# Two head pairs walk their WKV chunks together; low-rank products are made once, ahead of the heads

## The chip, the cores and the metric

One core of a Trainium2 chip runs the whole program, in one launch. The metric is the time of one execution on the device in microseconds; the kernel before takes 1480.89 us in the median of three runs (1479.6 to 1481.0).

## What is computed

The reference is one layer of a decoder for 512 prompt tokens and 8 samples of 8 tokens each, 576 columns in all: a SwiGLU feed-forward block, a mixing block, and a second feed-forward block. The mixing block has three branches (an RWKV-7 recurrence, a causal convolution, a cross-attention), each weighted by its own sigmoid gate, summed and projected. The change lies in the RWKV branch. Cut to that:

```python
wd, ad, gd = xm[..., c3:c4], xm[..., c4:c5], xm[..., c5:]           # 64, 64 and 160 wide
w_log = -jax.nn.softplus(-(p['w0'] + jnp.tanh(wd) @ p['w_decay_up'])) - 0.5
decay = jnp.exp(-jnp.exp(w_log))
a = jax.nn.sigmoid(p['a0'] + ad @ p['w_a_up'])
g = jax.nn.sigmoid(gd) @ p['w_g_up']
...
def step(s, inp):                                                    # per head, 64 x 64 state
    sa = jnp.einsum('bhij,bhj->bhi', s, -kk_t)
    s = (s * w_t[:, :, None, :] + sa[..., None] * kka_t[:, :, None, :]
         + v_t[..., None] * k_t[:, :, None, :])
    return s, jnp.einsum('bhij,bhj->bhi', s, r_t)
...
y_a = (o.reshape(b, t, D_RWKV) * g) @ p['w_rwkv_out']
```

There are 8 heads of 64 channels, handled as 4 pairs of 128 channels (one pair fills the 128 partitions).

## The kernel before, in words

Channels lie on partitions and the 576 tokens in the free dimension, in two halves of 288. A large product is made of three matmuls in the type fp32r: each operand is split into a rounded part and the rest (`split`, a ScalarE cast at L96 and a VectorE subtraction at L97), and the rest times the rest is left out. These matmuls are issued at L110 (`mm3k`, called by `proj`), 24 for each half and 1024 input channels, and at L382 in the feed-forward blocks. Small products are single matmuls in plain fp32, which the profile counts as two passes each (transposes as one).

The mixing block starts when the first feed-forward block ends. `lora` makes the inputs of three low-rank products (`la`, `lg`) by the projections 12, 13 and 14 of `w_in`. Then the string `PLAN` gives the order in which the pieces are written down, and the scheduler of the tile framework settles the order of each engine from it: A is the attention, P`j` the preparation of pair `j` (`prep`), I`j` the inverse of the 32 x 32 triangles (`inverse`, mostly VectorE), J`j` their joining into 64 x 64 (`joined`), B`j` the recurrence of pair `j` (`chain`), G and C the convolution, and X, Y, Z are the 24 gates, each a projection of 48 matmuls at L110 that depends on nothing else of the mixing. The gates fill TensorE while the other pieces wait for VectorE, ScalarE and each other.

`prep` makes in plain fp32 the products of `la` with `wda` for decay and for `a` (L128, `full`), and the masked Gram blocks (L893). `chain` transposes `kb` and `v` (L911, L915), runs `chunks`, then `sample_chunk`, and then the norm over each head. In the norm, the sums of squares are spread to all rows by matmuls at L148, and the product of `lg` with `wg` follows (L128 again, bank `c`); its result in PSUM multiplies the normed output. `chunks` walks the 8 chunks of 64 tokens of a pair one after the other. A chunk is one bank of PSUM and these matmuls, all for the two heads of one pair: values (L1024), the state's share (L1027), the solve (L1031), the update of the state (L1042), the output (L1057) and the state's share of the output (L1059). Between them stand two ScalarE copies (`xs` L1029, `vu` L1033), a scaled copy of the state (`mg` L1047) and VectorE's update (`st` L1051). The next chunk's L1027 needs the updated state.

Outputs of pairs 0 to 2 go to memory (`d_ya`) and come back before the merge, which multiplies all four by `w_rwkv_out`; its matmuls are the first at L110 that read `k`, `r`, `av`, `zt`, `w`, `g` and `u1`.

PSUM has three banks with the tag `p`, two with `g` and three with `c`. All loads and most stores are issued by SP's queue, in the order that the scheduler sets. Weights are loaded at L86 (`w<-win` and others) into two buffers of 1024 columns.

## Time and profile before

| what | value |
|---|---|
| median of three runs | 1480.89 us |
| the profiled execution, whole | 1484.21 us |
| its span, first to last instruction | 1482.4 us |
| its mean granted TensorE clock | 0.985 |
| TensorE busy | 1464.2 us, 10820 matmul passes |
| VectorE busy, ScalarE busy | 1026.1 us, 676.2 us |
| the mixing block up to the merge, about | 421 to 994 us of the span |

A page of the profile gives the busy time of each engine, the chain of waits that ended last, and groups of instructions by line. A busy TensorE is not a TensorE at its peak: a matmul's end is modelled, and a row's length covers its passage through the array. The distance from the start of one row to the start of the next tells what it held the engine for. "128*64" in a row is the part of the array that is used, rows by columns.

### The profile page before, as it was taken

Reading aid. Unit: us, or ns where it says so; the run is one execution under the profiler, and the core shown is the slowest. Engines: PE = TensorE matmul, PEld = TensorE weight load, DVE = VectorE, ACT = ScalarE, POOL = GpSimd, SP = SyncE. Lnnn points to the kernel's source line nnn. Section 1 sums busy time; section 2 is a strip of 40 time slices with the busy share of each in tenths; the row PEclk is TensorE's granted clock in tenths of the full one; section 3 lists DMA queues with packets and bytes.
Section 4 is the critical chain, followed back from the end, with each engine's and each line's share of the span. In section 5 each row is a group of like instructions: output and inputs, shape, how many; then the busy total and the mean of one; then the engine's idle time right before and its main releaser. Section 6 shows DMA issues by size and latency. Waiting matters only on the chain.

```text
span 1482.4 us, 27100 instructions
## 1 busy us (share of the span) xinstructions
PE 1464.2 (99%) x10820; PEld 1382.3 (93%) x10820; DVE 1026.1 (69%) x2054; ACT 676.2 (46%) x1371; POOL 4.7 (0%) x22
## 2 busy tenths in 40 slices
PE   9999999999999999999999999999999999999998
PEld 9999999999998799878889878789999999999997
DVE  7976777777783569769456456357578766777775
ACT  7443434444577535445446533443354433444342
POOL 0000000000010000000000000000000000000000
PEclk9999999999999989999999999999999999999999
DMA  6222222233632244123223124345322322323221
GB/s 210 72 80 92 87 86 86 86 91 102 202 105 86 65 132 83 55 80 105 62 61 109 55 85 137 96 161 189 102 73 72 100 73 85 100 89 98 86 86 65
DMA packets 95179, 144.06 MB, mean 97 GB/s; under 512 B 43645, under 2 KB 53501, under 8 KB 95053
## 3 DMA queue, kind: packets, MB, share of 16 engines
q1 hardware_dynamic: 94476, 141.74, 31.1%
q8 instruction: 85, 1.39, 0.4%
q10 hardware_dynamic: 576, 0.59, 0.1%
q14 instruction: 42, 0.34, 0.1%
HBM read 126.07 MB, written 16.23 MB: 96 GB/s over the span
## 4 chain that ended last, share of the span: by engine, by line
PE 92%; DVE 4%; ACT 1%; DMA 1%; issue 1%; SPq 0%; DVEq 0%; POOL 0%; ACTq 0%; POOLq 0%
PE p L110 51%; PE p L382 26%; PE c L1027 1%; PE g L893 1%; PE c L1031 1%; PE c L1024 1%; DVE pr L986 1%; PE c L128 1%; PE c L1059 1%; PE g L128 1%; PE c L1057 1%; DVE cc L676 1%; PE c L1079 1%; DVE tt L988 1%; PE c L1042 1%
## 5 line engine op out<-in xcount | busy, mean ns | idle before, releaser
L110 PE MATMUL p<-x,wh 128*128 128x288 f32 x3136 | 655.6, 300 | 1.3 <-ACT kv L562 0.7
L110 PEld LDWEIGHTS p<-x,wh 128*128 128x128 f32 x3136 | 507.2, 189 | 15.2 <-issue 7.1
L110 PE MATMUL p<-x,wl 128*128 128x288 f32 x1568 | 470.0, 300 | 1.5 <-DVE wl L97 1.5
L96 ACT CAST wh<-w 128x512 fp32r<-128x512 f32 (+1 forms) x353 | 209.8, 600 | 261.9 <-PE p L382 99.8
L97 DVE TENSOR_TENSOR wl<-w,wh 128x512 fp32r<-128x512 f32 (+1 forms) x353 | 232.4, 663 | 117.4 <-ACT wh L96 110.4
L110 PEld LDWEIGHTS p<-x,wl 128*128 128x128 f32 x1568 | 295.4, 189 | 7.1 <-issue 3.1
L382 PE MATMUL p<-t,wh 128*128 128x288 f32 x1088 | 224.3, 298 | 0.0
L382 PEld LDWEIGHTS p<-t,wh 128*128 128x128 f32 x1088 | 173.8, 188 | 6.4 <-DVE t L393 6.4
L382 PE MATMUL p<-b,wh 128*128 128x288 f32 x816 | 169.7, 295 | 0.0
L382 PE MATMUL p<-t,wl 128*128 128x288 f32 x544 | 160.6, 295 | 0.0
L96 ACT CAST wh<-p 128x512 fp32r<-128x512 f32 x136 | 84.5, 621 | 156.1 <-PE p L110 117.7
L382 PEld LDWEIGHTS p<-b,wh 128*128 128x128 f32 x816 | 132.6, 188 | 0.0
L97 DVE TENSOR_TENSOR wl<-p,wh 128x512 fp32r<-128x512 f32 x136 | 93.7, 689 | 50.1 <-ACT wh L96 47.4
L382 PE MATMUL p<-b,wl 128*128 128x288 f32 x408 | 120.3, 295 | 0.0
L382 PEld LDWEIGHTS p<-t,wl 128*128 128x128 f32 x544 | 102.4, 188 | 0.0
L382 PEld LDWEIGHTS p<-b,wl 128*128 128x128 f32 x408 | 76.8, 188 | 0.0
L460 DVE SCALAR_TENSOR_TENSOR x<-p,x 128x288 f32<-128x288 f32 x128 | 57.9, 453 | 20.0 <-PE p L110 19.9
L96 ACT CAST x<-t 128x576 fp32r<-128x576 f32 (+1 forms) x60 | 36.5, 610 | 45.0 <-DVE t L464 41.8
L1051 DVE SCALAR_TENSOR_TENSOR st<-c,gc,mg 64x64 f32<-64x64 f32 x56 | 15.9, 284 | 53.3 <-PE c L1042 52.5
L372 DVE TENSOR_TENSOR p<-w 128x512 f32<-128x512 f32 x68 | 46.7, 687 | 4.2 <-DMA w<-wu 3.8
L372 DVE TENSOR_TENSOR p<-p,w 128x512 f32<-128x512 f32 x68 | 46.5, 683 | 0.2 <-DMA w<-wu 0.2
L676 DVE SCALAR_TENSOR_TENSOR cc<-up,pv,cc 128x512 f32<-128x512 f32 x60 | 43.9, 750 | 0.1
(354 smaller groups left out, 1990.8 us busy)
## 6 DMA issues: line engine op xcount, KB each, us to landing
w<-wu SPq DMA_DIRECT2D x85, 512.0 KB
w<-win SPq DMA_DIRECT2D x44, 512.0 KB
w<-wd SPq DMA_DIRECT2D x64, 256.0 KB
w<-wd SPq DMA_DIRECT2D x16, 384.0 KB
d_mb<-gate SPq DMA_DIRECT2D x16, 288.0 KB
w<-wo SPq DMA_DIRECT2D x8, 512.0 KB
d_x<-x SPq DMA_DIRECT2D x16, 144.0 KB
d_g<-gate SPq DMA_DIRECT2D x8, 288.0 KB
```

Source lines behind the costliest of these rows:

```text
L96: self.A.copy(hi, x)
L97: self.V.tensor_tensor(lo, x, hi.bitcast(F32), ALU.subtract)
L110: self.T.matmul(p, l, x[r][:, c], start=k == 0 and i == 0, stop=k == n - 1 and i == 2)
L128: self.T.matmul(p, l, r[:, c], start=i == 0, stop=i == len(ops) - 1)
L372: V.tensor_tensor(s, u, v, ALU.add)
L382: self.T.matmul(p, hl[l][:, c], xs[k][b][:, o], start=first and k == 0 and q == 0, stop=k == 3 and q == 2, skip_group_check=True)
L460: V.scalar_tensor_tensor(x[m][:, c], p, 0.5, x[m][:, c], ALU.mult, ALU.add)
L676: V.scalar_tensor_tensor(c[:, :SEQ], up[:, k:k + SEQ], w, c[:, :SEQ], ALU.mult, ALU.add)
L893: T.matmul(ps[:, i * 128:(i + 1) * 128], kb[o, c + i].rearrange("p a t -> p (a t)"), ra[o, c + i].rearrange("p a t -> p (a t)"), start=Tru ...
L986: V.tensor_tensor(pr, tt[:, :n, :e].unsqueeze(2).broadcast_to([np_, n, m, e]), l3[:, t:e, :e].unsqueeze(1).broadcast_to([np_, n, m, e]), A ...
L988: V.tensor_reduce(tt[:, :n, t:e], pr, op=ALU.add, axis=AX.X)
L1051: V.scalar_tensor_tensor(mn[s, s], ps[s, 256 + 64 * h:320 + 64 * h], gc[s, c:c + 1], mg[s, s], ALU.mult, ALU.add)
```

## The change

The four recurrences become two: `chains(j)` takes pairs `j` and `j + 1` and walks both through each chunk together. One bank holds values, share of the state, solve and update of both; `xs` and `vu` are copied once, 256 wide; the outputs of both go to a bank of tag `g`. The state update is four products of 64 columns of `kbt` (L1143) instead of one of 128 columns for each pair. The values of the next chunk are issued right after the outputs. The sample chunk of each pair is cut into three pieces, and one piece is issued behind each of the first six chunks. The order of the matmuls within a chunk is partly fixed by `keep_in_program_order`.

The transposes move from the recurrence into `prep` (bank `g`). All low-rank products move to the beginning (`low_rank`): they become fp32r matmuls in parts (L677, 64 of 288 columns), and their results go to memory (`d_w`, `d_a`, `d_gt`) and are loaded where they are needed. For this `wda` is loaded twice over both halves of the partitions, and the 32 last rows of `lg` are made three times (96 rows in projection 14). `PLAN` is new. Only pairs 0 and 1 go to memory before the merge.

```diff
-PLAN = ("A0 P0 I0 Y3 G0 J0 P1 B0 Y1 I1 X2 Y1 X2 J1 P2 B1 "
-        "X1 I2 X2 C0 Y3 P3 J2 B2 X1 Z1 I3 Z3 J3 B3 Z2 L0 Z2")
+PLAN = ("A0 P0 I0 Y3 G0 P1 J0 I1 Y3 X1 J1 B0 X3 P2 I2 Y2 X2 P3 J2 X2 I3 C0 Z2 J3 B2 Z4 L0 Z2")
...
+    def low_rank(self, zp):
+        ...
+        def products(*ops):
+            for h in range(2):
+                c = slice(h * H, (h + 1) * H)
+                p = self.bank("g")[:, :H]
+                for q, (l, r) in enumerate(ops):
+                    T.matmul(p, l, r[:, c], start=q == 0, stop=q == len(ops) - 1)
+                yield c, p
+        for j in range(4):
+            ...
+                for c, p in products((wh[:, i, ch], xs[:, i]), (wl[o, ch], xs[o, i])):
+                    A.activation(t[:, c], p, AF.Sigmoid, bias=self.par(par, j))
+                self.store(out[j], t)
+            ...
+            for c, p in products((gh[:, 0, ch], lg[:, 0]), (gh[:, 0, ch], lg[:, 1]), (gl[:, ch], lg[:, 0]),
+                                 (gh[:96, 1, ch], gs[:96])):
+                A.copy(t[:, c], p)
+            self.store(self.d_gt[j], t)
...
-        for c, p in self.full("g", (self.wda[:64, 128 * j:128 * j + 128], self.la[:64])):
-            A.activation(sg[:, c], p, AF.Sigmoid, bias=par("w0", j))
+        self.dma(sg, self.d_w[j])
...
-        ch = slice(128 * j, 128 * j + 128)
-        for c, p in self.full("c", (self.wg[0][:, ch], self.lg[0]), (self.wg[1][:, ch], self.lg[1])):
-            V.tensor_tensor(rs[:, c], p, rs[:, c], ALU.mult)
+        gt = b3.tile([128, N], F32, name="gt")
+        self.dma(gt, self.d_gt[j])
+        V.tensor_tensor(rs, gt, rs, ALU.mult)
...
+    def chains(self, j):
+        samples = [s for i in (j, j + 1) for s in self.sample_chunk(i)]
+        self.chunks(j, lambda: samples and samples.pop(0)())
+        for i in (j, j + 1):
+            self.mixed(i)
...
+            xs = self.b3.tile([128, 256], F32, name="xs")
+            A.copy(xs[64:], ps[64:, :256])
+            for i, h, s in parts:
+                T.matmul(ps[64:, col(0, i, h)], made[i][0][64:, h, c, 64:], xs[64:, col(0, i, h)], start=True, stop=True)
+            A.copy(vb[64:, c].rearrange("p i v -> p (i v)"), ps[64:, :256])
+            for i, h, s in parts:
+                gr, kbt, vu, ra, gc, bv = made[i]
+                T.matmul(ps[s, 256 + 64 * i:320 + 64 * i], kbt[:, c, s], vu[:, c, s], start=True, stop=True)
+            mn = self.st[c % 3]
+            py = self.bank("g")
```

Three places show how the program's order moves. The first is TensorE within a chunk. Before, in the recurrence of pair 0, from one chunk's share of the state (L1027) to its update (L1042); L110 are the matmuls of a gate:

```order
L1027 MATMUL c<-st_5310,ra 64x128
L110 MATMUL p<-x_4953,wh 128x288
L110 MATMUL p<-x_4954,wh 128x288
L110 MATMUL p<-x_4953,wl 128x288
L1024 MATMUL c<-vu,gr 64x64 x2
L110 MATMUL p<-x_4955,wh 128x288
L1031 MATMUL c<-xs,gr 64x64 x2
L110 MATMUL p<-x_4956,wh 128x288
L110 MATMUL p<-x_4955,wl 128x288
L110 MATMUL p<-x_4957,wh 128x288
L1042 MATMUL c<-vu,kbt 128x128
L110 MATMUL p<-x_4958,wh 128x288
```

Now, in the recurrence of pairs 0 and 1, from the end of a run of gate matmuls (here at L109) over the update (L1143), the outputs (L1151, L1153), the next chunk's values (L1122) and a piece of a sample chunk (L1201) to the next share of the state (L1132):

```order
L109 MATMUL p<-x_4958,wh 128x288
L109 MATMUL p<-x_4957,wl 128x288
L1143 MATMUL c<-vu,kbt 64x64 x4
L1151 MATMUL g<-gr,vu 64x64 x2
L1153 MATMUL g<-ra,st_5315 128x64
L1151 MATMUL g<-gr,vu 64x64 x2
L1153 MATMUL g<-ra,st_5315 128x64
L1122 MATMUL c<-vu,gr 64x64 x4
L1201 MATMUL c<-u_8005,kbt 64x512
L1201 MATMUL c<-u_8008,kbt 64x512
L1132 MATMUL c<-st_5316,ra 64x128 x2
```

The groups have twice the matmuls, update, outputs and values stand together without a gate between them, and the gate matmuls stand in three runs.

The second is SP's queue behind the first recurrence. Before, around the store of pair 0's output (`d_ya_100`) and the next loads of weights:

```order
L809 DMA d_mb_85<-gate 128x576
L86 DMA w<-woc 128x256
L941 DMA d_ya_100<-u_7459 128x576
L86 DMA w<-win 128x1024
L248 DMA d_g_96<-gate 128x576
```

Now, with the stores of pairs 0 and 1 (`d_ya_100`, `d_ya_101`), the loads of `gt` (one buffer) and the next weights:

```order
L85 DMA w<-win 128x1024 x2
L1000 DMA d_ya_100<-u_8235 128x576
L996 DMA gt<-d_gt_113 128x576
L1186 DMA ms<-wst 64x8x64 x2
L863 DMA d_mb_89<-gate 128x576
L1000 DMA d_ya_101<-u_8271 128x576
L85 DMA w<-win 128x1024
```

A load of weights stands behind two stores and a load that wait for the end of the norms of both pairs.

The third is TensorE behind the last norm. Now, from pair 3's spread (L147) through the last gate matmuls:

```order
L147 MATMUL g<-cst,u_10747 128x128 x4
L147 MATMUL g<-cst,u_10747 128x64
L109 MATMUL p<-cb0h,wh 128x288
L109 MATMUL p<-cb0l,wh 128x288
L109 MATMUL p<-cb0h,wl 128x288
L109 MATMUL p<-cb1h,wh 128x288
L109 MATMUL p<-cb1l,wh 128x288
L109 MATMUL p<-cb1h,wl 128x288
```

Twelve matmuls of the last gate stand there (six are shown), then eleven of the merge that read pairs 0 to 2, and the next reads pair 3. Before, four matmuls at L128 and 44 at L110 stood between that spread and the merge.

## The prediction

> **What bounds the kernel now.** The page comes first: its busy times and the chain that ended last.

> ```profile
> span 1482.4 us, 27100 instructions
> PE   1464.2 (99%) x10820; PEld 1382.3 (93%) x10820; DVE 1026.1 (69%) x2054; ACT 676.2 (46%) x1371; POOL 4.7 (0%) x22
> PE 92%; DVE 4%; ACT 1%; DMA 1%; issue 1%; SPq 0%; DVEq 0%; POOL 0%; ACTq 0%; POOLq 0%
> ```

> TensorE is busy 99% and carries 92% of the chain. So the first question is what the change makes TensorE do, and only then who waits. The change touches the mixing block alone, so next come the stretches of that block (span, TensorE busy, weight loads, VectorE, ScalarE, GpSimd, granted clock, DMA share, GB/s), and the chain's own rows where gate and merge matmuls run dense.

> ```profile
> 421.00:994.00 573.00, 563.13 (x4103) 489.22 (x4102) 354.64 (x809) 284.04 (x663) 4.26 (x15) 0.96 0.32 92
> 720.00:740.00 20.00, 19.89 (x128) 16.15 (x128) 5.50 (x14) 8.85 (x21) 0.00 (x0) 0.83 0.17 46
> 1438.42 22.22 PE p L110 x168
> ```

> A dense fp32r matmul of 288 columns holds TensorE for 22.22/168 = 0.132 us. In the mixing TensorE is idle in only 10 of 573 us, but it isn't dense: the small matmuls hold it much longer than their columns need. The timeline of one chunk of pair 0 shows how (start, length, line; the distance between starts is what counts).

> ```profile
> 621.04 0.34 PE L1057 MATMUL c<-gr,vu 128*64 128x64 f32 x4
> 621.30 0.43 PE L1059 MATMUL c<-ra,st 128*128 128x64 f32 x2
> 621.67 0.43 PE L1027 MATMUL c<-st,ra 128*64 128x128 f32 x2
> 622.03 0.53 PE L110 MATMUL p<-x,wh 128*128 128x288 f32 x2
> 622.40 0.29 PE L110 MATMUL p<-x,wl 128*128 128x288 f32 x1
> 622.62 0.44 PE L1024 MATMUL c<-vu,gr 64*64 64x64 f32 x4
> 622.99 0.40 PE L110 MATMUL p<-x,wh 128*128 128x288 f32 x1
> 623.32 0.44 PE L1031 MATMUL c<-xs,gr 64*64 64x64 f32 x4
> 623.69 0.40 PE L110 MATMUL p<-x,wh 128*128 128x288 f32 x1
> 623.93 0.30 PE L110 MATMUL p<-x,wl 128*128 128x288 f32 x1
> ...
> 624.20 0.40 PE L1042 MATMUL c<-vu,kbt 128*128 128x128 f32 x2
> 624.36 0.38 PE L110 MATMUL p<-x,wh 128*128 128x288 f32 x1
> 624.58 0.29 PE L110 MATMUL p<-x,wl 128*128 128x288 f32 x1
> ...
> 625.60 0.28 PE L1057 MATMUL c<-gr,vu 128*64 128x64 f32 x2
> ```

> From L1057 to the next L1057 are 4.56 us, with fifteen matmuls of L110 in them, which dense would take 15 x 0.132 = 1.98 us. The chunk step therefore holds TensorE for 2.58 us. The two groups of 64*64 take 0.37 us each, and the first gate matmul behind a group 0.24 (623.69) or 0.33 (622.99) instead of 0.132: each change of the part of the array that is used costs 0.1 to 0.2 us.

> Does the recurrence's own chain of waits limit it instead? Two rows of the groups say no: TensorE waited 0.4 us in all for the updated state, VectorE's update 52.5 us for TensorE.

> ```profile
> L1057 PE MATMUL c<-gr,vu 128*64 128x64 f32 x128 | 10.9, 249 | 0.4 <-DVE st L1051 0.4
> L1051 DVE SCALAR_TENSOR_TENSOR st<-c,gc,mg 64x64 f32<-64x64 f32 x56 | 15.9, 284 | 53.3 <-PE c L1042 52.5
> ```

> **The change part by part.** *Low-rank products.* Those of decay and `a` go from `prep`, those of `g` from behind the norm; the second row below is one of four pairs'.

> ```profile
> L128 PE MATMUL g<-la,wda 64*128 64x288 f32 x32 | 9.4, 442 | 0.5 <-ACT u L827 0.5
> 984.34 2.72 PE c L128 x8
> ```

> Removed: 9.4 + 4 x 2.72 = 20.3 us. Added: 64 fp32r matmuls of 288 columns, dense 64 x 0.132 = 8.5 us. Sixteen of them use 64 rows of the array and stand between others that use 128. At 0.1 us for the way in and 0.1 out they cost 3.2 us more, at 0.2 each 6.4 us, at nothing 0. I take 3.2, since a group that keeps the columns and changes the rows is nearer to the cheap switches. Gain 8.6 us, bounds 5.4 and 11.8. [...]

> *Chunks of two pairs together.* Thirty-two single steps become sixteen double ones. A double step has twice the passes, but most groups keep one switch. What a pass adds inside a group is shown by runs of equal passes: ten of L1027 in 1.23 us, 0.12 each, and those of 64*64 at 0.06.

> ```profile
> 636.80 1.31 PE L1027 MATMUL c<-ms,ax 128*64 128x128 f32 x10
> 638.03 0.44 PE L1031 MATMUL c<-xs,gr 64*64 64x64 f32 x4
> 752.08 0.22 PE L1024 MATMUL c<-vu,gr 64*64 64x64 f32 x1
> 752.14 0.22 PE L1024 MATMUL c<-vu,gr 64*64 64x64 f32 x1
> ```

> To 2.58 us come: values 4 x 0.06, solve 4 x 0.06, share of the state 2 x 0.12, that is 0.72; outputs a second time with their switch, 0.26 + 0.37 = 0.63; and the update, now eight passes of the form of L1057, whose four take 0.26, so 0.52 instead of the 0.25 that its two held TensorE (0.38 from 624.20 to 624.58, less one L110), 0.27 more. The double step holds TensorE 4.20 us, two single ones 5.16: 0.96 saved, sixteen times 15.4 us. Two of the sixteen are first steps without state terms, and pieces of sample chunks stand inside some groups and split them, so I take 12 us; the bounds are 0 (each doubled group costs double) and 15.4. The halved ScalarE copies (`xs`, `vu`) gain nothing by themselves: ScalarE is at 284 of 573 us in this block. The rest of the step's waits gets more cover, since the fillers per double step stay about fifteen.

> *Transposes.* The same 72 on the same engine, now in a bank of `g` instead of `c`; 0 us. Gate matmuls hide the copies; without that cover two banks instead of three cost up to the length of a copy, twelve times for each kind, which I count below.

> *The beginning.* Sixteen sigmoids and eight copies out of PSUM and the splits move to where the mixing starts; two banks of `g` serve all of them.

> ```profile
> L827 ACT ACTIVATE u<-g,pv 128x288 f32<-128x288 f32 x8 | 3.9, 501 | 2.3 <-PE g L128 2.2
> 440.00:460.00 20.00, 20.00 (x137) 17.77 (x135) 6.85 (x17) 11.13 (x28) 0.53 (x1) 1.00 0.41 135
> ```

> Twenty-four at about 0.5 us are 12 us of ScalarE. It has 9 us free in those 20, and the products and the projections between them last about 28 us by count (118 gate or projection matmuls, 15.6, and 11.7), so it fits with little room. I take 2 us lost, bounds 0 and 8 (the 12 us less half the free time).

> *The end.* Before, the last low-rank product and 31 gate matmuls stood between pair 3's spread and the merge. Now twelve do, and eleven of the merge itself: 23 x 0.132 = 3.0 us of cover.

> ```profile
> 987.05 4.32 PE p L110 x31
> L935 DVE TENSOR_TENSOR u<-u,bv 128x576 f32<-128x576 f32 x4 | 3.0, 748 | 0.6 <-ACT u L934 0.6
> L97 DVE TENSOR_TENSOR u<-u,u 128x576 fp32r<-128x576 f32 x1 | 0.8, 759 | 0.7 <-ACT u L96 0.7
> ```

> Behind the spread come six operations over 576 columns in a row (scale, affine, sum, gate, cast, rest), at about 0.75 us each 4.5 us. 1.5 us are late; bounds 0 and 4.5.

> *SP's queue.* A load of weights now stands behind the stores of both pairs' outputs and behind `gt`, whose one buffer is free only after the first norm; the gate matmuls behind it on TensorE wait. The longest wait for weights in this block, on the chain of waits, is the upper bound:

> ```profile
> 575.33 7.71 DMA w<-win
> ```

> With the banks of `g` I take 2 us, bounds 0 and 8.

> Sum: -8.6 - 12 + 2 + 1.5 + 2 = -15.1 us. The profiled execution took 1484.21 us (1482.4 in the span and 1.8 around it), 3.3 more than the median of 1480.89. The sum holds for either: 1469.1 for an execution like the profiled one, and 1480.9 - 15 = 1466 us for the median, my forecast.

> **The rivals.** *Slower: the clock.* Between 720 and 740 us TensorE is busy 19.89 of 20 us and is granted 0.83 of its clock; dense stretches have 1.00. So small matmuls without enough dense ones between them lower the clock, and over the block 0.04 of 573 us is lost, some 20 us. The change packs the small groups: update, outputs and values stand together, and a sample piece among them. A double step with fifteen fillers lasts 4.20 + 1.98 = 6.2 us, sixteen 99 us. If 0.83 held in all of them, they would take 99/0.83 = 119 us, 20 more than forecast: 1486 us. It decides below a mean of 0.87 in these stretches (99/114). Against it: a double step has a third of its time in dense matmuls, and the single step of 4.56 us that is shown has not much more. [...]

> *No change: the groups don't share.* If each doubled group costs double, only the low-rank products gain, and the beginning, the end and the queue take most of it: -8.6 + 5.5 = -3.1, 1478 us; with a little more lost it is no change. For it speaks that every switch between parts of the array remains inside the outputs; against it the 0.06 and 0.12 us above.

> *Less gain: ScalarE bounds the beginning, or the queue starves TensorE.* At one of the ends of 8 us the total is 1472 us.

> *More gain.* Chunk steps at 15.4 us, nothing lost at either end, and half of the 10 us in which TensorE is idle in this block gone: -8.6 - 15.4 - 5 = -29, 1452 us.

> **How the numbers follow.** About 0.2% (3 us) can be told from no change. Chances: the forecast within 1459 to 1470, 0.42; less gain, 1470 to 1478, 0.23; more gain, 0.14; no change, 0.07; slower by the clock, 0.14. Faster: 0.79. The range leaves out the half of "more" beyond its own value and most of "slower", and takes in the no-change case: 1452 to 1482 us.

> **What would show it.** Right: the products at L677 hold TensorE 11 to 12 us in all; from one update at L1143 to the next are about 6 us, with fifteen gate matmuls, 4.2 us after their dense time; TensorE idle no more than 15 us in the mixing; clock about 0.96 there. Wrong: a clock under 0.87 around the two recurrences (the slower rival), a double step of over 5 us beside its fillers (no sharing), idle TensorE of 5 us or more before the attention (ScalarE) or behind the first recurrence (SP's queue).

## The result and the profile after

The changed kernel takes 1493.23 us in the median of six runs (1489.63 to 1500.19) against 1481.05 (1479.6 to 1484.77): a ratio of 1.0088, 95% interval 1.0059 to 1.0118. It is slower, and 27 us from the forecast of 1466. Its profiled execution took 1491.07 us, that of before 1484.21.

The page of the changed kernel, the same three rows as shown of before:

```profile
span 1489.2 us, 27301 instructions
PE   1449.4 (97%) x10884; PEld 1384.6 (93%) x10884; DVE 1028.1 (69%) x2059; ACT 664.4 (45%) x1348; POOL 5.0 (0%) x22
PE 90%; DVE 6%; issue 1%; ACT 1%; DMA 1%; SPq 0%; DVEq 0%; POOL 0%; ACTq 0%; POOLq 0%
```

TensorE is busy 14.8 us less, and the span is 6.8 us longer. VectorE has 6% of the chain instead of 4%. The stretches of the changed kernel (columns as before: span, TensorE, weight loads, VectorE, ScalarE, GpSimd, clock, DMA share, GB/s) say where:

```profile
420.00:1001.00 581.00, 549.34 (x4166) 492.37 (x4164) 356.49 (x812) 272.13 (x637) 1.55 (x4) 0.94 0.33 98
704.00:760.00 56.00, 56.00 (x513) 45.11 (x511) 18.50 (x44) 19.48 (x64) 0.00 (x0) 0.97 0.14 38
840.00:860.00 20.00, 14.39 (x74) 13.93 (x75) 11.82 (x23) 10.49 (x15) 0.00 (x0) 0.71 0.32 79
860.00:880.00 20.00, 14.48 (x137) 13.75 (x136) 8.57 (x30) 5.86 (x13) 0.00 (x0) 0.76 0.42 120
900.00:920.00 20.00, 11.44 (x119) 10.71 (x120) 4.11 (x8) 4.17 (x10) 0.00 (x0) 0.75 0.44 115
917.00:980.00 63.00, 62.54 (x516) 50.48 (x513) 23.71 (x55) 22.58 (x67) 0.00 (x0) 0.85 0.20 53
```

In the block TensorE is idle 31.7 us (581 less 549.3; before 9.9) and has 0.94 of its clock (before 0.96). Most of the idle time gathers between the first recurrence (704 to 760 us, never idle, clock 0.97) and the second (917 to 980, hardly idle, clock 0.85). The windows at half clock lie more widely: they cost 35.8 us in the block by half their length, 15 of these between the two recurrences and 12 from 917 us on. TensorE's longest waits in the block (us in total, times, longest), first of the changed kernel, then of before:

```profile
PE p L109 <- DVE wl L96: 6.7, 5, 3.2
PE c L1067 <- DMA aux<-s: 6.1, 1, 6.1
PE p L109 <- ACT cb0h L95: 5.4, 1, 5.4
```

```profile
PE c L1008 <- DMA aux<-s: 2.0, 1, 2.0
PE p L110 <- DVE wl L97: 1.5, 3, 1.1
```

L1067 is the joining of pair 3, which needs pair 3's inverse. `wl` is the rest part of a gate's weights: VectorE makes it, so the fillers themselves queue up behind the inverse's operations there. Pieces of the chain of waits ahead of it (start, length, what):

```profile
828.70 0.55 DVE pr L1045
...
850.79 0.72 DVE pr L1045
...
856.23 0.66 ACT cb0h L95
...
882.21 0.65 DVE pr L1045
...
909.38 3.07 DMA aux<-s
912.49 1.93 PE c L1067 x32
```

VectorE makes the inverse of pair 2 (816 to 852 us) and then that of pair 3 (873 to 901). Before, the inverse of pair 3 (863 to 912 us) went on beside the recurrence of pair 2 (840 to 884) and its norm. Now both inverses, the joinings and the convolution's tail (`cb0h`) must be done before the second recurrence starts.

To see all of it at once, I split the mixing, from its first matmul to the merge, in three: idle time (distances between the starts of two matmuls of over 0.9 us, each less one dense matmul), time lost at half clock (half the length of the windows at 0.5, as far as TensorE was not idle in them, so that nothing counts twice), and the rest, which is work. It is an estimate from the starts of the matmuls and the granted clock in the traces: in the mixing of the changed kernel a dense gate matmul holds TensorE 0.133 us at 1.00 and 0.240 at 0.50 (medians of 1,923 and 93), so such matmuls lose 0.45 of a window's length, a little less than half. Medians are those of each kernel's runs; the profiled times belong to the split.

| kernel | median | profiled | mixing | half clock | idle | rest |
|---|---|---|---|---|---|---|
| before | 1481.05 | 1484.21 | 571.8 | 18.3 | 10.9 | 542.5 |
| changed | 1493.23 | 1491.07 | 580.0 | 29.6 | 33.3 | 517.1 |
| changed_again | 1501.72 | 1505.83 | 594.0 | 46.3 | 31.1 | 516.6 |
| low_rank_alone | 1498.79 | 1501.11 | 588.0 | 29.6 | 22.1 | 536.3 |
| pairing_alone | 1519.99 | 1521.28 | 604.6 | 49.9 | 30.3 | 524.5 |
| two_inverses | 1478.96 | 1486.73 | 574.1 | 40.1 | 15.4 | 518.6 |
| fewer_terms | 1467.87 | 1471.02 | 559.2 | 22.5 | 21.5 | 515.3 |

The rows changed, changed_again and two_inverses have the same work on TensorE, and their rest agrees within 2 us. The work fell by 25.4 us, more than the 20.6 forecast. Idle time rose by 22.4 and half clock by 11.3: the mixing is 8.2 us longer.

### The profile page after: what moved, and what is told of

It is laid out like the page before. It is cut to its first block, busy times and chain, and to the rows that moved or that the text cites. A ratio compares the mean times of both kernels' runs of the same rounds, so it can differ in the third digit from the quotient of the medians.

```text
span 1489.2 us, 27301 instructions
## 1 busy us (share of the span) xinstructions
PE 1449.4 (97%) x10884; PEld 1384.6 (93%) x10884; DVE 1028.1 (69%) x2059; ACT 664.4 (45%) x1348; POOL 5.0 (0%) x22
## 4 chain that ended last, share of the span: by engine, by line
PE 90%; DVE 6%; issue 1%; ACT 1%; DMA 1%; SPq 0%; DVEq 0%; POOL 0%; ACTq 0%; POOLq 0%
PE p L109 50%; PE p L384 26%; DVE pr L1045 2%; DVE tt L1047 1%; PE g L945 1%; DVE wl L96 1%; PE g L677 1%; PE c L1122 1%; PE g L1153 1%; PE c L1139 1%; PE g L137 1%; DVE cc L730 1%; PE c L1086 1%; PE g L147 1%; PE c L1132 1%
## 5 line engine op out<-in xcount | busy, mean ns | idle before, releaser
L109 PE MATMUL p<-x,wh 128*128 128x288 f32 x3136 | 653.7, 301 | 4.2 <-ACT wh L95 3.5
L109 PEld LDWEIGHTS p<-x,wh 128*128 128x128 f32 x3136 | 511.8, 191 | 12.4 <-ACT wh L95 4.2
L109 PE MATMUL p<-x,wl 128*128 128x288 f32 x1568 | 472.0, 302 | 6.8 <-DVE wl L96 6.7
L109 PEld LDWEIGHTS p<-x,wl 128*128 128x128 f32 x1568 | 298.5, 191 | 12.9 <-DVE wl L96 8.7
L96 DVE TENSOR_TENSOR wl<-w,wh 128x512 fp32r<-128x512 f32 (+1 forms) x354 | 232.5, 662 | 109.8 <-ACT wh L95 99.5
L96 DVE TENSOR_TENSOR wl<-p,wh 128x512 fp32r<-128x512 f32 x136 | 93.6, 688 | 50.6 <-ACT wh L95 47.8
L851 ACT ACTIVATE gate<-p 128x288 f32<-128x288 f32 x48 | 19.7, 410 | 55.9 <-PE p L109 50.6
```

The source lines that it names most:

```text
L96: self.V.tensor_tensor(lo, x, hi.bitcast(F32), ALU.subtract)
L109: self.T.matmul(p, l, x[r][:, c], start=k == 0 and i == 0, stop=k == n - 1 and i == 2)
L851: self.A.activation(g[:, c], p, AF.Sigmoid)
```

## Experiments

**The two halves alone.** In `low_rank_alone` the recurrences and `PLAN` are those of before; in `pairing_alone` the low-rank products are (loaded in slices, for room):

```diff
-        self.dma(sg, self.d_w[j])
+        for c, p in self.full("g", (wda[:64], self.la[:64])):
+            A.activation(sg[:, c], p, AF.Sigmoid, bias=par("w0", j))
```

> The kernel before with the low-rank part of the change alone: products once at the beginning in fp32r, their results through memory, the order of the pieces and the single-pair recurrences as before. Cover theory (the loss comes from the pairing, which takes away the recurrence that covered the last inverse): the products of L677 hold TensorE 14 us as in the changed kernel, so 20.3 - 14.1 = 6 us are saved, 2 to 3 us go at the start of the mixing and 1 to 2 us at its end: 1476 to 1480 us, against 1481 before; idle TensorE in the mixing stays under 16 us. Beginning theory (ScalarE's work at the beginning and the loads and stores of its results on SP's queue make the loss): 1488 us or more, with 20 us or more of idle TensorE. Clock theory: as the cover theory, since the recurrences are as before.

> The changed kernel with the low-rank products as before (plain fp32, in the preparation and behind the norm, their weights loaded in slices for each pair), and u2 in two buffers instead of three. The first four experiments brought down the theory that only the last inverse's lost cover counts, since the low-rank part alone cost 18 us. Front theory: the low-rank products, 28 us of TensorE's order at 444 to 472 us and 16 sigmoids, 8 copies and the splits on ScalarE and VectorE, stand ahead of pair 0 in the chain of pieces; its Gram blocks come 21 us later (499 to 520 us) and its joining 33 us (575 to 608). Then without them Gram is back near 500, J of pair 0 near 580, and the time is 1493 less some 18: 1468 to 1480 us. Cover theory alone (the pairing loses): 1488 us or more.

Measured: 1498.79 us (ratio 1.0126, 1.0093 to 1.0159) and 1519.99 (1.0260, 1.0227 to 1.0293). My cover theory missed the first, and the front theory, formed on the first, missed the second: pair 0's joining did come back to 574 us, and the time rose. The work behaves as a sum: 542.5 before, 536.3 with low-rank products changed (-6.2), 524.5 with pairing (-18.0), 517.1 with both (-25.4). The time does not. Each half alone loses 18 and 39 us, the two together 12. Idle time rises by 11.2 and 19.4 us in the halves, half clock by 11.3 and 31.6. So neither half "costs" a fixed amount. That each shifts work away from where it covered a wait would fit this, but the halves alone don't show it; `pairing_alone` also has less room (`u2` in two buffers, weights loaded for each pair), and that was not separated. In `low_rank_alone` the 64 products stand at 444 to 472 us, ahead of pair 0; its joining comes at 608 us instead of 575, and all later ones 12 to 23 us later. In `pairing_alone` the plain fp32 products of `g` stand behind each recurrence, at the end uncovered: the last four hold TensorE from 1023 to 1028 us, right ahead of the merge at 1029 (changed: merge at 1001).

`half_front` moves only the products of decay and `a`:

> The changed kernel with the products of decay and a at the beginning as changed (32 of the 64), those of g as before behind the norm. Front theory: half the delay, Gram of pair 0 near 510 and its joining near 590 us, and the time between pairing_alone's and the changed kernel's: 1478 to 1488 us. If the delay comes from elsewhere (the loads of decay and a through memory): Gram at 518 to 522 and 1488 to 1496.

Measured 1506.53 us (1.0151, 1.0096 to 1.0205). Gram came at 503 to 514 us, but the joining of pair 0 only at 600. The time lies between the changed kernel's and `pairing_alone`'s, as expected, but `pairing_alone` turned out to be the slow end, and the expected 1478 to 1488 us are missed. The front theory is dropped.

**Is removed work saved?** The same kernel as before, with less in the gates:

```diff
+        self.terms = 3 - i % 2
         for c, p in self.proj(self.a["win"][20 + 8 * n + i], self.xn):
```

> The kernel before with less work on TensorE and nothing else moved by hand: in 12 of the 24 gates the third of the three products (the rest of the weights times the input) is left out, 192 matmuls of 0.132 us, 25.3 us of the mixing. If what is taken from TensorE comes off the time in full, as the prediction's sum had it: 1456 us (1452 to 1460). If the chain of pieces (VectorE's inverses, ScalarE, loads) stands close behind TensorE, a third or more comes back as idle time or as half clock: 1464 to 1476 us, and idle and half clock in the mixing rise from 31 us to 40 or more.

Measured 1467.87 us (0.9910, 0.9888 to 0.9933). Of 25.3 us taken from TensorE 13.2 came off. The block and TensorE's longest wait in it:

```profile
421.00:981.00 560.00, 542.69 (x3907) 468.01 (x3906) 352.77 (x809) 281.84 (x662) 4.26 (x15) 0.95 0.32 93
PE c L1013 <- DMA aux<-s: 3.6, 1, 3.6
```

By the split, idle time rises from 10.9 to 21.5 us and half clock from 18.3 to 22.5, and the longest wait is again the one for the last inverse. This needs no pairing and no new order: a 99% busy TensorE had other chains close behind it.

**The chain ahead of the second recurrence.** The odd pairs' inverse gets free buffers:

```diff
-        lt = b1.tile([128, 1024], F32, name="lt")[:np_]
+        lt = self.room(j, "lt", "kb", 1152)[:np_, :1024]
```

> The changed kernel with the work tiles of the inverse of the odd pairs in other, then free buffers (kb, v, k), so that the inverse of pair 3 need not wait until that of pair 2 has left lt, tt and pr. Cover theory: VectorE starts pair 3's inverse near 852 us rather than at 873 and the second recurrence starts some 15 us earlier than 917; of the 24 us in which TensorE is idle between 837 and 917 some 15 go, and the half-clock windows that follow idle go with them (5 us): 1471 to 1478 us. Clock theory (the small matmuls packed into the double steps lower the clock, idle or not): the time lost at half clock stays at 38 to 42 us, only idle goes: 1478 to 1484. Beginning theory: 1490 to 1495, nothing changes where the loss is.

> The changed kernel without the inverse of pair 3 (its triangles stay as they are; that part of the computation is left out, and its 30 us of VectorE and its loads and stores with it). Cover theory: all idle time behind 870 us goes (3.6, 2.4, 6.4 and 1.2 us, with 3 us more near it) and the half-clock windows at 872 and 910 us, some 13 of the 27 us that they last: 1468 to 1476 us. Clock theory: idle goes, half clock stays at 38 to 42 us lost: 1476 to 1481. Beginning theory: 1490 to 1495.

Measured 1478.96 us for `two_inverses` (0.9985, 0.9954 to 1.0016) and 1484.22 for `no_inverse_3` (1.0020, 0.9993 to 1.0047). In the changed kernel pair 3's inverse could begin when `lt` was free and `sub` copied; with its own buffer it begins 26 us earlier, in the midst of pair 2's. The first row is of the changed kernel, the second of `two_inverses` (start, length, instruction):

```profile
873.31 0.07 DVE L1037 MEMSET lt<- 108x11 f32 x1 [3.54 <-ACT sub L1036]
```

```profile
847.09 0.07 DVE L1044 MEMSET kb<- 108x11 f32 x1
```

The second recurrence starts at 897 instead of 917 us, and idle time falls from 33 to 15 us. 14 us of the median come back with TensorE's work unchanged (two more sets of runs of the same kernel, below, gave 1483.20 and 1484.15), and the kernel is level with before. So the lost cover of the inverse is shown to make most of the idle time. It is not all: with 24 us less work than before, `two_inverses` should have been faster, and half clock takes that gain (40.1 us against 18.3). Of the three theories the clock's came nearest. It expected 1478 to 1484 us and 38 to 42 us at half clock; the half lengths of the windows, as the expectation counts them, sum to 41.0 us. Leaving the inverse out gave less than any theory expected; its recurrence starts at 881 us, but the gates then run out behind it (one wait of 6.4 us near 959).

**The order of the pieces.** Four kernels move the convolution's tail or the joinings; three of them on top of `two_inverses`:

```diff
-... B0 X3 P2 I2 Y2 X2 P3 J2 X2 I3 C0 Z2 J3 B2 Z4 L0 Z2
+... B0 X3 C0 P2 I2 Y2 X2 P3 J2 X2 I3 Z2 J3 B2 Z4 L0 Z2    conv_first
+... B0 X3 P2 I2 Y2 X2 P3 C0 J2 X2 I3 Z3 J3 B2 Z3 L0 Z2    conv_tail_earlier
+... B0 X3 P2 C0 I2 Y2 X2 P3 J2 X2 I3 Z3 J3 B2 Z3 L0 Z2    gates_between
+... B0 X2 P2 I2 Y2 X3 P3 C0 I3 J2 X2 Z3 J3 B2 Z3 L0 Z2    joins_together
```

> The changed kernel with one move in PLAN: the convolution's tail (C0) is written right behind the first recurrence rather than behind the inverse of pair 3. TensorE waited 5.7 us at 851 us for cb0h, the convolution's output, and half-clock windows followed. Cover theory in its narrow form (the inverse chain of pairs 2 and 3 sets the start of the second recurrence whatever else stands there): that wait goes, but the chain is no shorter and the idle time moves behind it: 1487 to 1494 us. If the gates' order is the cause (the fillers were there, but in the wrong order): the 5.7 us and 5 us of half clock go, 1480 to 1485. Clock and beginning theories: 1490 to 1495.

> two_inverses with C0 in front of the joining of pair 2 and three gates Z rather than two ahead of the last joining. In two_inverses TensorE still waited 5.3 us at 856 us for cb0h and ran 6.8 us at half clock behind it. Cover theory: that wait and its half clock go (8 us): 1468 to 1474 us, faster than before by 0.5 to 0.9%. If the wait only moves to the last joining: 1475 to 1482.

> two_inverses with C0 right behind the preparation of pair 2; the scheduler then sets three gates between the joinings of pairs 2 and 3 instead of two, and the second recurrence has one less beside its sample pieces. Cover theory: the wait for cb0h goes, the second recurrence starts with TensorE busy: 1466 to 1476 us. If the convolution's tail ahead of pair 2's chain pushes that chain back, as in conv_first: 1485 to 1500, and pair 2's Gram blocks come after 805 us.

> two_inverses with the inverse of pair 3 written ahead of the joining of pair 2, so that both joinings stand together with all gates ahead of them. Cover theory: the gates cover both inverses, but nothing stands between the two joinings (64 passes of 32 columns each), which are too sparse for the clock: the wait for cb0h goes (8 us), 5 us come back at half clock: 1472 to 1480. If only the order of the fillers counts, not their density: 1464 to 1472.

Measured 1513.51 us (1.0232, 1.0186 to 1.0278), 1486.19 (1.0040, 1.0028 to 1.0053), 1489.65 (1.0066, 1.0043 to 1.0088) and 1497.86 (1.0115, 1.0079 to 1.0151). None beats its base, and none bears out its expectation: only `gates_between` falls into a stated range, and the condition of that range (pair 2's Gram blocks after 805 us) was not met, they come at 792 to 801. `conv_first` put pair 2's Gram blocks at 819 us instead of 792, and the chain behind them as late. In the others the wait for `cb0h` went, and another came in the same stretch: 4.9 us for `wl` at 873, 5.3 for pair 3's inverse at 906, 7.1 for `wl` at 891. The wait moved each time.

**Both remedies at once.**

> The same with the odd pairs' inverse in buffers of its own (as in two_inverses). Front and cover theory together, if the two losses add: 1479 less 18, 1455 to 1468 us, faster than before by 1% or more, with no more than 15 us of idle TensorE in the mixing. If they are two sights of one wait: as pairing_alone, within 4 us.

Measured 1503.34 us (1.0153, 1.0123 to 1.0184): 17 us better than `pairing_alone`, which speaks again for the inverse's buffers, but neither expectation holds: the two did not add to a gain over before.

```profile
746.20:749.60 3.40, 3.40 (x39) 3.04 (x38) 0.70 (x3) 0.36 (x2) 0.00 (x0) 1.00 0.02 5
749.60:753.00 3.40, 3.40 (x31) 3.04 (x30) 1.72 (x4) 0.90 (x5) 0.00 (x0) 1.00 0.01 2
753.00:756.40 3.40, 3.40 (x15) 1.51 (x14) 1.37 (x2) 1.01 (x3) 0.00 (x0) 0.50 0.00 0
```

They hold 3,552, 1,568 and 3,136 columns: the second is sparse, the third runs at half. Two kernels add dense matmuls in the double steps:

```diff
+        x = self.xn[0][0]
+        for _ in range(n):
+            self.tc.keep_in_program_order(self.T.matmul(p[:, 128:416], x[:, :128], x[:, :H], start=True, stop=True,
```

> two_inverses with four matmuls more in each double step, fp32r of 288 columns into a part of the outputs' bank that nobody reads: two behind the update, two behind the outputs. They are 64 x 0.132 = 8.5 us of work with some 4 us of changes of the array's part. Clock theory, in the form that six traces gave: a window of 3.41 us in which TensorE starts less than about a third of the columns that it could is followed by a window at half clock, where the same work fills half as much, so the low state keeps itself up; whether a double step falls below is chance, and two_inverses ranges from 1469 to 1498 us for it. With the filling the half clock inside the two recurrences goes (17 us or more were lost there in the profiled run of two_inverses), and the runs lie within 10 us of each other, 1474 to 1486. If the clock has another cause: 12 us more than two_inverses in the median, 1491, with the same spread.

> two_inverses with 36 such matmuls ahead of the wait for cb0h and four more in the double steps 0, 1 and 7 of both recurrences, where single windows were below a third (60 in all, 7.9 us, 4.8 of them in idle time). Density theory: half clock at 860, inside the first recurrence and behind its steps 0 and 1 goes, 10 us or more against 3 us of work and some changes of the array's part: 1466 to 1476 us, faster than before by 0.4% or more. If the added work counts in full and the clock doesn't follow it: 1482 to 1488.

Measured 1503.05 us (1.0153, 1.0102 to 1.0204) and 1487.50 (1.0031, 1.0008 to 1.0054). Both miss their clock theories; the second lies where the expectation has the added work count in full. In `two_inverses_filled` half clock in the first recurrence did go, and its profiled execution was granted 0.980 of the clock over the span (`two_inverses` 0.970); in `dense_steps` (0.973) it stayed at the end of the first recurrence (757 to 774 us), behind matmuls of 8 columns of a sample piece. The added work counted in full or more: the medians lie 8.5 us above the 1478.96 of `two_inverses` for 7.9 us of it, and 24.1 us above for 8.5 and an estimated 4 of changes. The third kernel adds work only where TensorE was idle:

> The changed kernel with work added: 80 dense fp32r matmuls of 288 columns (10.6 us) whose result nobody reads, 36 ahead of the wait for cb0h at 851 us, 44 behind the joining of pair 2, where TensorE is idle for 5.6 and some 13 us. Density theory of the clock (a window of 3.41 us with less than a third of the columns that TensorE could stream is followed by one at half clock): idle time falls by 10 us and the work rises by as much, and the half-clock windows that followed the idle (at 855, 872 and 910 us, 34 us long) get fewer: 1482 to 1490 us, faster than the changed kernel in spite of more work. If half clock does not come from sparse windows: 1493 to 1500.

Measured 1493.93 us (1.0075, 1.0041 to 1.0108), no faster than the changed kernel, though idle time in the mixing fell from 33 to 20 us. By the time alone that is the range of the other theory, in which half clock does not come from sparse windows. In place the filling shows. The wait of the changed kernel at 851 us, and the window behind it:

```profile
851.30:856.80 5.50, 0.24 (x2) 0.01 (x1) 2.70 (x7) 5.12 (x8) 0.00 (x0) 0.87 0.28 51
856.80:863.60 6.80, 6.67 (x32) 6.62 (x33) 3.34 (x6) 2.73 (x5) 0.00 (x0) 0.60 0.67 130
```

and the same stretch in `fill_idle`, which comes there about 7 us later in its own program:

```profile
856.80:863.60 6.80, 6.80 (x53) 6.61 (x51) 3.89 (x8) 4.38 (x6) 0.00 (x0) 1.00 0.20 37
863.60:870.00 6.40, 5.71 (x43) 5.48 (x43) 3.29 (x6) 3.92 (x7) 0.00 (x0) 1.00 0.57 79
```

Filled, the place runs at 1.00, and the half clock behind the wait (855 to 862 us in the changed kernel) is gone. That ahead of it stays (842 to 849 us there, 849 to 856 here), and the profiled execution has half clock at other places too, 17 us of windows within the first recurrence, for one, where the changed kernel's first profile had 3.4. Whether the clock could be won back as a whole stays open: no run here does it.

**One program, three executions.**

> two_inverses once more, for a second profiled execution of the same program: its executions lie between 1469 and 1498 us. Density theory of the clock: chance decides in which double steps a window falls below a third, so the time lost at half clock differs from the first profile's 41 us in the mixing, the windows that differ lie in the two recurrences, and the two profiled times differ by as much as the lost times do (within 3 us), with the idle gaps the same within 3 us. If waits (loads, other engines) make the spread: idle gaps differ by more than 5 us and the lost time doesn't.

> A third profiled execution of the same program, with the same expectation: time less the time lost at half clock agrees over the three executions within 4 us; idle gaps do too.

The same 13 us of the first recurrence of `two_inverses`, in its three profiled executions:

```profile
717.00:730.00 13.00, 13.00 (x72) 10.28 (x72) 1.13 (x4) 2.97 (x11) 0.00 (x0) 0.50 0.01 1
```

```profile
717.00:730.00 13.00, 13.00 (x109) 10.45 (x109) 2.56 (x9) 3.18 (x12) 0.00 (x0) 0.87 0.00 1
```

```profile
717.00:730.00 13.00, 13.00 (x75) 10.73 (x74) 1.70 (x6) 2.98 (x11) 0.00 (x0) 0.50 0.00 1
```

TensorE is busy throughout, yet does 72, 109 and 75 passes. The executions took 1486.73, 1485.15 and 1495.42 us with 45.5, 44.3 and 59.4 us lost at half clock over the whole program; less that they are 1441.2, 1440.9 and 1436.0, 5.2 apart where 4 were expected (4.0 if half clock in idle time is left out). Idle time is 15.4, 16.2 and 15.1 us. The runs without a profile say the same, since each has its granted clock on record. Taken off the time, (1 - clock) x span estimates what the clock cost. Then 23 executions of `two_inverses` of 1469 to 1495 us come to 1437 to 1447, ten of the changed kernel of 1490 to 1506 us to 1450 to 1454, and twenty of before of 1477 to 1486 us to 1459 to 1463. So the clock makes the spread, and waits do not. The changed kernel once more:

> The changed kernel as it is, for a second profiled execution and more times. If idle time is the lasting part of the loss and half clock the one that varies: idle time in the mixing 33 us within 3, with the waits near 851 and 906 us again, half clock 25 to 50 us lost, and the median 1488 to 1498. If the idle time of the first profile was chance: under 25 us.

Measured 1501.72 us (1.0118, 1.0087 to 1.0150), above the expected range; idle 31.1 us with waits of some 5.4 us at 858 and 914 again, half clock 52.9 as the expectation counts it, above its 25 to 50. Less the half clock outside idle time, the profiled execution of before is at 1462.8 us, those of the changed kernel at 1457.5 and 1455.5: its work and its waits together would be a gain of 5 to 7 us, and the clock takes more than that.

**The rows of the low-rank products.**

```diff
-                for c, p in products((wh[:, i, ch], xs[:, i]), (wl[o, ch], xs[o, i])):
+                for c, p in products((wh[:, i, ch], xs[:, i]), (wl[:, i, ch], xs[:, i])):
```

> The changed kernel with wl widened to 128 rows (its other half zero), so that none of the 64 products of L677 uses half of the array's rows. In the changed kernel the sixteen with 64 rows hold TensorE 0.326 us each and those next to them 0.257, 14.1 us in all. If the change of rows makes that: 64 x 0.132 to 0.140, 8.5 to 9 us in all. If the reading of weights or the products' order makes it: 12 us or more.

One execution, 1508.31 us. First the changed kernel, where a product with 64 rows holds TensorE from 447.74 to 448.07 us, 0.33; then `full_rows`, from 451.56 to 451.69, 0.13:

```profile
447.52 0.30 PE L677 MATMUL g<-xs,wh 128*128 128x288 f32 x1
447.74 0.39 PE L677 MATMUL g<-xs,wl 64*128 64x288 f32 x1
448.07 0.40 PE L109 MATMUL p<-x,wh 128*128 128x288 f32 x1
```

```profile
451.56 0.29 PE L679 MATMUL g<-xs,wl 128*128 128x288 f32 x1
451.69 0.33 PE L679 MATMUL g<-xs,wh 128*128 128x288 f32 x1
```

The median of the sixteen falls from 0.326 to 0.137 us, so the change of rows is the cause. Yet all 64 still hold TensorE 13.5 us instead of 14.1. Some of them now wait for an operand and for ScalarE to empty the banks (`PE g L679` waits 0.9 us for `gs`, 1.7 for `bv`), and a window at half clock from 463.5 to 466.9 us falls among them, 1.7 us by half its length. The sum stays over 12 us for these reasons, so it does not speak for the reading of weights or the products' order, as the expectation would have it.

## Why the prediction was wrong, point by point

*The step that failed* is the first one: "TensorE is busy 99% and carries 92% of the chain. So the first question is what the change makes TensorE do, and only then who waits." The sum then counted removed work as saved time. `fewer_terms` measures what that is worth in this kernel: 13.2 of 25.3 us. In the sum's own terms, work was to fall by 20.6 us and fell by 25.4; waits were to cost 5.5 us and idle time rose by 22.4; the clock had no term, and half clock outside idle time rose by 11.3. Idle time is the larger miss. By this split the mixing would not have grown without the idle time, nor without the half clock.

The list of covers looked at the beginning, the end and the queue, and said of the recurrence only that its waits get more cover. It did not ask what each single recurrence covered for others, which was the next pair's inverse on VectorE. That cover's loss is most of the 22.4 us of idle time, and `two_inverses` gets 18 of them back. "What would show it" had the sign, 5 us or more of idle time behind the first recurrence, but gave it to SP's queue; the waits were for the inverse, for `wl` behind it and for the convolution's output.

*Low-rank products.* Forecast -8.6 us, with 11.7 held by L677. Held were 14.1, so 20.3 - 14.1 = 6.2 us saved, inside the bounds; the rest of `low_rank_alone` says the same. The mis-sized part is the change of rows: the product itself takes 0.19 us more, and the two next to it 0.1 each. The end of the bounds with 5.4 us saved was the nearer one.

*Chunk steps.* Forecast 4.20 us for a double step and 12 us in all. From one update to the next in the changed kernel:

```profile
728.08 0.45 PE L1143 MATMUL c<-vu,kbt 128*64 128x64 f32 x8
...
734.88 0.30 PE L109 MATMUL p<-x,wl 128*128 128x288 f32 x1
735.10 0.45 PE L1143 MATMUL c<-vu,kbt 128*64 128x64 f32 x8
```

7.02 us with 22 matmuls of L109 between, dense 2.90: 4.12 us, with four matmuls of a sample piece among them. Six steps without such a piece have 3.85 to 3.88, beside 14 to 18 gate matmuls. The mechanism was right and the gain larger: 18.0 us of work by `pairing_alone`, beyond the bound of 15.4.

*Beginning, end, queue.* A gap of 1.9 us at 437 waits for ScalarE, as forecast (2). One of 1.7 stands ahead of the merge, where 1.5 were forecast, but that is luck. The forecast had the merge wait for the six operations behind pair 3's spread; the row puts the wait down to VectorE's product with the last gate (L858), which reads a bank of TensorE (before, 0.62 us in the same place), and the first matmul that reads pair 3, at 1002.62, does not wait.

```profile
1001.09 0.37 PE L109 MATMUL p<-k,wh 128*128 128x288 f32 x1 [1.49 <-DVE gate L858]
```

Before, 43 gate matmuls stood in the trace between spread and merge; the prediction's 31 leave out twelve that read the convolution's output, and its sum does not use the number. The queue's 2 us were looked for in the wrong place: the rest parts of the weights do come late, 6.7 us in five waits, but for VectorE's order, since `wl` stands behind the inverse.

*The slower rival* named the clock and gave 1486 us at 0.14. The direction was right, the place only in part: the recurrences have 0.97 and 0.85, their mean above the 0.87 from which it was to decide, and 15 of 36 us lie between the recurrences, where the idle time is. It was weighed as an alternative to waits, where both came together.

## What to carry to other kernels

A busy share of 99% says that the fillers suffice, not that the engine is the only bound: before counting removed work as saved, ask of each piece that is merged or moved what it covered, and follow the chains of the other engines to the next join. A cheap test is to take a known amount of filler away and see how much of it comes off. Test both halves of a change, but do not expect them to add: here 18 and 39 us alone made 12 together. And where small matmuls are packed together, count their columns as well as the busy time: here TensorE was busy for 3.40 of 3.40 us from 749.6 us on, with 1,568 columns, and was granted 0.50 in the window behind.

## What was not expected of the hardware

In these traces half clock followed windows with few columns, with idle time in them or without. The counts are over 20 profiled executions, from 421.5 us to the merge, on the grid that the clock's changes give; a window has 3.41 us and counts the columns of the passes that start in it. At full clock, 152 of 166 windows with fewer than 2,700 columns were followed by a window at half clock, and 44 of 2,757 with more (11 of 2,590 above 3,440). Of the 166 sparse windows 77 had no gap of over 0.9 us between the starts of matmuls, and 65 of these were followed by half clock. Of 36 windows above 3,440 columns with more than 1 us of idle time, none was. The line at 2,700 was drawn on the first six traces and held on the other fourteen (111 of 119 below it). It describes these programs: columns are the one measure that was counted; another measure of sparse work, such as rows of the array, was not set against it, what the clock itself goes by was not shown, and no run that filled sparse windows gained time by it.

Half clock often went on: of 288 windows at half clock under 2,700 columns 235 were followed by another, of 108 above 3,440 only 3. The same work fills fewer columns there: the 13 us of `two_inverses` above have 72 and 75 passes at 0.50 and 109 at 0.87. That the state keeps itself up in this way would fit the counts, and no run tests it. The windows of the changed kernel's first recurrence hold 1,632 to 4,768 columns, on both sides of 2,700. That would fit why one program's executions differ by some 20 us (`two_inverses`, nine of its first ten from 1468.86 to 1487.53) where those of the kernel before differ by 5 to 10; why a window falls on one side in one execution and on the other in the next was not shown.
